# A rotary-embedding score kernel rewritten in emission order: three VectorE operations per rotation, no GpSimd, 4 MB stores, paired loads

## The chip, the cores and the metric

The kernel runs on one core of one Trainium2 chip. The metric is the device time of one execution in microseconds (us). The kernel before takes 897.9 us in the median of 4 runs (897.11 to 898.37). An execution with the profiler on lasts about as long as one without; "span" is the time from its first to its last instruction.

Some words that recur: a packet is one of the pieces (4 to 32 KB here) in which the core's 16 DMA engines move a transfer, and the trace has the start and duration of each; the ring is the queue in which transfers wait in the order of their issue; a transfer has landed when its last engine has reported completion; a stage is a buffer in SBUF (the core's on-chip memory) in which a step's output is collected before it is stored; PSUM is the memory into which TensorE writes, in banks; the granted clock is the share of TensorE's full clock rate that the profile shows.

## The reference

```python
batch, seq, heads, dim = 16, 512, 16, 64          # q, k: float32; cos, sin: [seq, dim/2]
q_rot = concat([q1*cos - q2*sin, q1*sin + q2*cos])   # q1, q2: the halves of dim
k_rot = the same of k
scores = einsum('bshd,bthd->bsht', q_rot, k_rot)     # [16, 512, 16, 512] float32
```

The output is 268.4 MB, the inputs 67.1 MB. A step of the kernel makes one batch's scores for 128 rows of q: 1 MB of loads (k and q, for later steps) and 4 MB of stores. There are 64 steps.

## The kernel before

Tiles come from pools, and a scheduler chooses each engine's order. q is rotated on VectorE and k on GpSimd, with six instructions of 128x512 each:

```python
kq_pool = ctx.enter_context(tc.tile_pool(name="kq", bufs=3))
stage_pool = ctx.enter_context(tc.tile_pool(name="stage", bufs=2))
...
return [lambda: eng.tensor_tensor(o1, x1, cb, op=mult),   # eng: vector for q, gpsimd for k
        lambda: eng.tensor_tensor(tmp, x2, sb, op=mult),
        lambda: eng.tensor_tensor(o1, o1, tmp, op=subtract),
        ...                                              # three more for o2
```

In each step, 16 matmuls go through four PSUM banks, ScalarE copies each bank to one of two 2 MB stages, and the transposes for the next steps come after them:

```python
rope_k = k_rope(rope_target(i), nc.gpsimd)
rope_q = q_rope(i + 2, nc.vector)
k_dma(rope_target(i + 2))            # nc.sync.dma_start, 512 KB
q_dma(i + 4)                         # nc.sync.dma_start, 512 KB
for h in range(H):
    nc.tensor.matmul(out=psm, ...)
    _cp(nc.scalar, sta[:, h, :], psm)                 # or stb
    ...  # after h = 7 and h = 15: nc.sync.dma_start of 2 MB
run_all(rope_k); run_all(rope_q)
do_transposes(specs, (nc.vector, nc.scalar))          # 16 transposes, 16 copies of 128x128
```

All transfers are issued by SyncE, so they stand in one ring in the order of issue.

## Time and profile before

| before | value |
|---|---|
| time, span | 897.9 us, 900.3 us |
| all DMA packets, sum over 16 engines / 16 | 840.7 us |
| DMA idle, span less that sum | 59.6 us |
| of it before the first store packet at 64 us | 39.1 us |
| load packets: 4 KB, median and mean | 159, 188 ns |
| store packets: 16 KB, median and mean | 611, 627 ns |

### The profile page before, as it was taken

The numbers are of one execution on the slowest core, as the hardware profiler recorded it, in microseconds if no ns is written. First come the engines' busy times: TensorE is split into PE (matmuls) and PEld (weight loads), VectorE is DVE, ScalarE is ACT, GpSimd is POOL, SyncE is SP. The second block draws the span as 40 slices with busy tenths as digits, with TensorE's granted clock in tenths as the row PEclk, the third lists the DMA queues.
The fourth block names the chain that finished last, engine by engine and source line by source line (L and its number), as shares of the span: only waits on it lengthen the run. The fifth ranks groups of instructions, "written<-read, shape, count | busy, mean of one in ns | idle before, by whom it ended". The sixth has DMA issues, their size and how long they took to land.

```text
span 900.3 us, 9994 instructions
## 1 busy us (share of the span) xinstructions
PE 718.8 (80%) x3072; PEld 408.7 (45%) x3072; DVE 573.8 (64%) x908; ACT 623.2 (69%) x1537; POOL 555.2 (62%) x378
## 2 busy tenths in 40 slices
PE   0367988987868878887988888888878988888994
PEld 0234544544535544444544544444445545545552
DVE  4997864454347776776775767775576566786500
ACT  0136977876757776766766867767767767767994
POOL 6993667655656766865866766777567674773000
PEclk9997999999989998999999989989989988989997
DMA  4358999999999999999999999999999998998998
GB/s 159 103 183 323 405 418 414 412 398 407 399 401 363 398 385 380 397 405 380 393 379 381 393 380 406 427 416 381 397 397 359 405 392 359 389 416 364 399 415 363
DMA packets 38068, 336.32 MB, mean 374 GB/s; under 512 B 5248, under 2 KB 5248, under 8 KB 21632
## 3 DMA queue, kind: packets, MB, share of 16 engines
q1 hardware_dynamic: 38016, 335.69, 93.1%
q8 instruction: 25, 0.41, 0.2%
q14 instruction: 27, 0.22, 0.1%
HBM read 67.24 MB, written 268.44 MB: 373 GB/s over the span
## 4 chain that ended last, share of the span: by engine, by line
DMA 40%; POOL 28%; PE 12%; DVE 10%; ACT 7%; issue 1%; SPq 1%; POOLq 0%; ACTq 0%; DVEq 0%
DMA ksb<-in_k_dram 21%; DMA qsb<-in_q_dram 19%; PE psm L205 11%; POOL krot L64 6%; POOL krot L65 6%; POOL krot L62 6%; POOL tmp L66 6%; POOL tmp L63 5%; ACT stb L76 3%; ACT sta L76 3%; DVE tmp L63 2%; PE bank L158 1%; DVE qrot L62 1%; DVE tmp L66 1%; DVE qT_new L78 1%
## 5 line engine op out<-in xcount | busy, mean ns | idle before, releaser
L205 PE MATMUL psm<-kT_new,qT_new 64*128 64x512 f32 x2048 | 592.7, 677 | 133.6 <-DVE qT_new L78 82.1
L205 PEld LDWEIGHTS psm<-kT_new,qT_new 64*128 64x128 f32 x2048 | 294.5, 200 | 393.6 <-ACT sta L76 161.1
L76 ACT COPY sta<-psm 128x512 f32<-128x512 f32 x512 | 267.1, 617 | 28.2 <-PE psm L205 27.5
L76 ACT COPY stb<-psm 128x512 f32<-128x512 f32 x512 | 262.1, 706 | 0.0
L63 DVE TENSOR_TENSOR tmp<-qsb,sin 128x512 f32<-128x512 f32 x64 | 65.4, 1021 | 239.5 <-DMA qsb<-in_q_dram 239.5
L63 POOL TENSOR_TENSOR tmp<-ksb,sin 128x512 f32<-128x512 f32 x62 | 88.6, 1429 | 194.3 <-DMA ksb<-in_k_dram 194.3
L76 ACT COPY qT_new<-bank 128x128 f32<-128x128 f32 x256 | 62.7, 267 | 191.2 <-DVE qT_new L78 190.0
L62 POOL TENSOR_TENSOR krot<-ksb,cos 128x512 f32<-128x512 f32 x62 | 92.1, 1486 | 65.8 <-PE bank L158 58.8
L78 DVE COPY qT_new<-bank 128x128 f32<-128x128 f32 x256 | 67.9, 284 | 53.1 <-PE bank L158 41.3
L65 POOL TENSOR_TENSOR krot<-ksb,sin 128x512 f32<-128x512 f32 x62 | 98.6, 1591 | 0.0
L64 POOL TENSOR_TENSOR krot<-krot,tmp 128x512 f32<-128x512 f32 x62 | 97.2, 1568 | 0.0
L76 ACT COPY kT_new<-bank 128x128 f32<-128x128 f32 x256 | 65.3, 266 | 46.0 <-DVE kT_new L78 45.0
L66 POOL TENSOR_TENSOR tmp<-ksb,cos 128x512 f32<-128x512 f32 x62 | 93.6, 1509 | 4.6
L67 POOL TENSOR_TENSOR krot<-krot,tmp 128x512 f32<-128x512 f32 x62 | 92.2, 1487 | 3.8
L158 PE MATMUL bank<-ident,krot 128*128 128x128 f32 x512 | 70.0, 282 | 28.0 <-POOL krot L67 18.3
L65 DVE TENSOR_TENSOR qrot<-qsb,sin 128x512 f32<-128x512 f32 x64 | 88.1, 1377 | 0.0
L67 DVE TENSOR_TENSOR qrot<-qrot,tmp 128x512 f32<-128x512 f32 x64 | 83.9, 1311 | 1.6
L66 DVE TENSOR_TENSOR tmp<-qsb,cos 128x512 f32<-128x512 f32 x64 | 82.8, 1293 | 0.0
L158 PEld LDWEIGHTS bank<-ident,qrot 128*128 128x128 f32 x512 | 55.5, 142 | 56.2 <-issue 56.2
L64 DVE TENSOR_TENSOR qrot<-qrot,tmp 128x512 f32<-128x512 f32 x64 | 80.7, 1261 | 0.0
L158 PE MATMUL bank<-ident,qrot 128*128 128x128 f32 x512 | 70.8, 282 | 8.1 <-DVE qrot L67 8.1
L158 PEld LDWEIGHTS bank<-ident,krot 128*128 128x128 f32 x512 | 60.6, 145 | 29.1 <-POOL krot L67 18.7
(15 smaller groups left out, 155.2 us busy)
## 6 DMA issues: line engine op xcount, KB each, us to landing
out_dram<-sta SPq DMA_DIRECT2D x64, 2048.0 KB, 10.0
out_dram<-stb SPq DMA_DIRECT2D x64, 2048.0 KB, 13.4
ksb<-in_k_dram SPq DMA_DIRECT2D x64, 512.0 KB, 5.8
qsb<-in_q_dram SPq DMA_DIRECT2D x64, 512.0 KB, 13.6
cos<-in_cos_dram SPq DMA_DIRECT2D x4, 16.0 KB, 1.8
sin<-in_sin_dram SPq DMA_DIRECT2D x4, 16.0 KB, 1.8
```

What stands on the lines that cost most here:

```text
L62: lambda: eng.tensor_tensor(o1, x1, cb, op=mybir.AluOpType.mult),
L63: lambda: eng.tensor_tensor(tmp, x2, sb, op=mybir.AluOpType.mult),
L64: lambda: eng.tensor_tensor(o1, o1, tmp, op=mybir.AluOpType.subtract),
L65: lambda: eng.tensor_tensor(o2, x1, sb, op=mybir.AluOpType.mult),
L66: lambda: eng.tensor_tensor(tmp, x2, cb, op=mybir.AluOpType.mult),
L67: lambda: eng.tensor_tensor(o2, o2, tmp, op=mybir.AluOpType.add),
L76: nc.scalar.copy(out=dst, in_=src)
L78: eng.tensor_copy(out=dst, in_=src)
L158: nc.tensor.transpose(slot, inap, ident)
L205: nc.tensor.matmul(out=psm, lhsT=qT[64 * r : 64 * r + 64, hp, :], rhs=kT[64 * r : 64 * r + 64, hp, :, :], start=True, stop=True,)
```

## The change

The intent: let program order fix every engine's order; make fewer, larger instructions and transfers; keep more output in flight. The core of the diff, with cuts:

```diff
-    kq_pool = ctx.enter_context(tc.tile_pool(name="kq", bufs=3))
-    rot_pool = ctx.enter_context(tc.tile_pool(name="rot", bufs=3))
+    in_pool = ctx.enter_context(tc.tile_pool(name="in", bufs=2))
+    rot_pool = ctx.enter_context(tc.tile_pool(name="rot", bufs=2))
-    stage_pool = ctx.enter_context(tc.tile_pool(name="stage", bufs=2))
-    psum_t_pool = ctx.enter_context(tc.psum_pool(name="ps_t", bufs=4))
-    psum_m_pool = ctx.enter_context(tc.psum_pool(name="ps_m", bufs=4))
+    stage_pool = ctx.enter_context(tc.tile_pool(name="stage", bufs=3))
+    ps_s_pool = ctx.enter_context(tc.psum_pool(name="ps_s", bufs=3))
+    ps_t_pool = ctx.enter_context(tc.psum_pool(name="ps_t", bufs=2))
+    q_v = q.rearrange("b (p c) h d -> b p c h d", c=C)
+    k_v = k.rearrange("b (c p) h d -> b p c h d", p=P)
+    o_v = out.rearrange("b (p c) h t -> b c p h t", c=C)
 ...  (tables of cos|cos and sin|-sin, loaded from ScalarE's ring)
+        t = in_pool.tile([P, 2, H, D], fp32, tag="k_in", bufs=3, name="k_sb")
+            nc.sync.dma_start(t, k_v[b, :, 2 * pair : 2 * pair + 2])     # 1 MB; q the same, bufs=2
 ...
+            lambda: nc.vector.tensor_tensor(a, src, cc, op=mult),
+            lambda: nc.vector.tensor_tensor(bt, src, ss, op=mult),
+            lambda: nc.vector.tensor_tensor(a4, a4, swapped, op=add),
 ...
+    with tc.manual_schedule():
 ...
+            after = {0: 0, 2: 1, 3: 2, 5: 3}
+            for hp in range(HP):
+                ps = ps_s_pool.tile([P, 2, S], fp32, tag="ps_s")
+                for r in range(2):
+                    nc.tensor.matmul(out=ps[:, r, :], ...)
+                nc.scalar.copy(out=st[:, 2 * hp : 2 * hp + 2, :], in_=ps)
+                if hp in after and after[hp] < len(tr):
+                    rot, g, dst = tr[after[hp]]
+                    bank = transpose_group(rot, g)
+                    if dve:
+                        dve.pop(0)()
+                    nc.vector.tensor_copy(out=dst, in_=bank)
+            for op in dve:
+                op()
 ...  (one 1 MB load: q in odd steps, k in even ones)
+                nc.sync.dma_start(o_v[b, c], st)                          # 4 MB
```

## The prediction

> **What bounds the kernel now.** I read the page first (busy shares, slices, DMA table), then the stretches of time, the packet records, the start of the timeline and the groups of instructions. The slices and the queue table carry most of it:
>
> ```profile
> PE 718.8 (80%) x3072; PEld 408.7 (45%) x3072; DVE 573.8 (64%) x908; ACT 623.2 (69%) x1537; POOL 555.2 (62%) x378
> ...
> DMA  4358999999999999999999999999999998998998
> GB/s 159 103 183 323 405 418 414 412 398 407 399 401 363 398 385 380 397 405 380 393 379 381 393 380 406 427 416 381 397 397 359 405 392 359 389 416 364 399 415 363
> ...
> q1 hardware_dynamic: 38016, 335.69, 93.1%
> ```
>
> No compute engine is above 80%, while the 16 DMA engines are at 90% or more in every slice but the first four and a few late ones that read 8. The chain that ended last is 40% "DMA" and 28% "POOL", which looks like a latency loop (load, GpSimd rotation, buffer free, next load); but the stretches say that the pipe it waits on is full:
>
> ```profile
> core 0: us, PE busy (x) PEld busy (x) DVE busy (x) ACT busy (x) POOL busy (x), PEclk, DMA share, GB/s
> 0.00:60.00 60.00, 20.82 (x72) 13.10 (x72) 47.06 (x49) 13.07 (x36) 52.08 (x38) 1.00 0.37 129
> 60.00:100.00 40.00, 29.55 (x128) 16.78 (x128) 32.96 (x49) 25.08 (x65) 23.08 (x15) 0.83 0.88 337
> 100.00:200.00 100.00, 85.52 (x385) 49.17 (x383) 57.21 (x114) 76.76 (x193) 60.77 (x47) 0.98 1.01 413
> ...
> 400.00:500.00 100.00, 83.04 (x355) 46.39 (x352) 72.00 (x103) 72.48 (x181) 69.52 (x45) 0.95 0.98 387
> ```
>
> The last two columns are the busy share of the DMA engines and the rate. From 100 us on the share is 0.92 to 1.01, so the steady state is DMA time. Idle is in the front: 0.63 x 60 = 38 us and 0.12 x 40 = 5 us. Of the span of 900.3 us, 93.1% or some 838 us is packet time, so about 62 us in all is idle.
>
> The rate at a full share is not constant: 413 GB/s in the second 100 us, 387 between 400 and 500. Counting the packet records by size shows why. The 16,384 store packets of 16 KB have a median of 0.611 us and a mean of 0.627; the 16,384 load packets of 4 KB have a median of 0.159 and a mean of 0.188, with a tail up to 1.6 us. By medians the work would take 16,384 x 0.611 / 16 + 16,384 x 0.159 / 16 = 626 + 163 = 788 us; by means it is 642 + 193 = 835. So 47 us is stretched packets, 30 of them on loads. The long load packets come just after stores. In 100 to 150 us, where work is queued ahead, the loads average 22.6 GB/s per engine; in 400 to 450 us, where the queue runs nearly empty before a load is issued, 18.8.
>
> **What the Trainium skill says.** "VectorE: DVE Perf Modes", section "The TRN2 errata", gives a fp32 tensor_tensor of N elements (N+151)/0.96 ns, so 691 ns at 512. "SBUF — State Buffer", section "Who interferes with whom", says that a VectorE instruction with two SBUF inputs contends with a GpSimd instruction that reads SBUF. The trace has both. The first of these rows has GpSimd waiting for its load, the second has it running:
>
> ```profile
> 410.56 0.69 DVE L63 TENSOR_TENSOR tmp<-qsb,sin 128x512 f32<-128x512 f32 x1 [2.42 <-DMA qsb<-in_q_dram]
> ...
> 403.05 1.75 DVE L65 TENSOR_TENSOR qrot<-qsb,sin 128x512 f32<-128x512 f32 x1
> ```
>
> "DMA: Bandwidth & Descriptors", section "Latency and other measured facts", lists 16 KB rows at a pitch of 512 KiB at nearly full rate and of 2 MiB clearly slower. The new store has 32 KB rows at a pitch of 4 x 32 = 128 KB, which that list does not reach, and the old one had 32 KB pitch, so no run here shows it yet. That all stores and loads share one ring is as it was before, so I give it no gain.
>
> **The change part by part.**
>
> *Rotation.* Six VectorE and six GpSimd instructions of 128x512 per step become six VectorE instructions of 128x1024 (three for q, three for k). Without GpSimd I take the 0.69 us row and add 512 elements at 1/0.96 ns: 1.22 us each, as the page's formula gives (1.224); back to back some 1.17, because the rows of 0.69 follow one another at 0.61. Six are 7.0 us.
>
> *PSUM copies of the transposes.* Sixteen 128x128 copies per step, half on VectorE (0.284 us) and half on ScalarE (0.267), become four 128x512 VectorE copies: 0.284 + 384/0.96 ns = 0.68, say 2.7 us. VectorE's step: 9.7 us.
>
> *Score copies.* Sixteen of 128x512 per step become eight of 128x1024. Now the row
>
> ```profile
> 405.19 4.11 ACT L76 COPY stb<-psm 128x512 f32<-128x512 f32 x8
> ```
>
> gives 0.51 us each. Adding 512 elements at the 0.833 ns of "ScalarE: Activation LUTs", section "Step-by-step: what each stage is for", makes 0.94, and 8 x 0.94 = 7.5 us per step against the 16 x 0.51 = 8.2 plus 2.1 of before. These rows agree only loosely with 0.833: 0.51 less 0.25 (three 128x128 copies in 0.75) over 384 elements is 0.68 ns.
>
> *TensorE.* The same matmuls: 16 at 0.43 us where it is not held by ScalarE (weight loads of 879.94, 880.48, 880.91 follow at that distance), 6.9 us, and 16 transposes at 8 per 1.05 us, 2.1 us. 9 us.
>
> So every engine needs under 10 us per step, and the pieces are interleaved so that they mostly overlap; I expect a compute step of about 10 us.
>
> *DMA.* The same 335.5 MB. From the medians of 4 KB and 16 KB packets a packet costs 8 ns plus 0.0368 ns per byte (an estimate), so 8,192 stores of 32 KB take 1.214 us each, 621 us in all; 8,192 k packets of 4 KB 81 us; 4,096 q packets of 8 KB at 0.310 us, 79 us; about 2 us for semaphores and tables. Floor: 783 us, 5 less than before. That is 12.2 us per step, above the 10 us of compute, so three stages of 4 MB keep one to two stores queued ahead all the time. I therefore use the loss of the stretch with a full queue: 100 to 150 us moves 407 GB/s at a share of 0.996, 409, against 425.5 by medians: 0.961. 783 / 0.961 = 815 us of packet time.
>
> *The start.* The old kernel spends 4.5 us of SyncE issue on eight tables before k; the first k lands at 8.1 us. Now tables go out from ScalarE and k at once: k lands at some 4.3 us, with tables built near 4.6. VectorE then rotates alone: four k chunks 14.0, q tables 1.1, q 3.5, q 3.5, k of the next batch 3.5 us: 30.2 us. Step 0 cannot transpose before that, and its own VectorE work is 9.7 us, so the first store leaves at about 40.5 us. By then 8.4 MB of loads are done, 20.4 us of packets. The end is 40.5 + (815 - 20.4) + 2 for the last landing = 837 us of span. The span of before is 2.6 us longer than the timed median, so 834 us timed. I move it up to 838 since more can stretch than shrink.
>
> So the gain of about 60 us is some 40 us of DMA idle time (62 down to about 22) and some 20 us of packet time (835 down to 815). The shorter rotation itself is worth nothing after the start: it only keeps VectorE alone below the DMA's step.
>
> **Rivals.**
> 1. *The pipe is full anyway and loads stay slow.* A load after each 4 MB store still pays; k and q come in 1 MB bursts, as in 400 to 450 us, where 384.6 GB/s at a share of 0.988 make 389. Then packet time is 783 x 425.5 / 389 = 856, the end 878 us, timed 876: 2.4% faster. For it: the long packets sit in those bursts. Against it: there the queue was nearly empty, and will not be now.
> 2. *VectorE becomes the bound.* All rotation and all transpose copies are on one in-order engine, and its first rotation in each step waits for a q load. If a pair of operations waits for the other engine at each of four transposes, a step of 14 us is thinkable: 40 + 63 x 14 = 922 us, 3% slower. For it: TensorE waits for VectorE at each new step. Against it: 9.7 us leaves 3 us per step, two PSUM banks hold transposes, and each q pair is issued two whole steps (25 us) ahead.
> 3. *The pitch of the stores costs rate.* Each 3% lost on the 621 us of stores is 19 us; 10% would give back all of the gain.
> 4. *Loads ahead of stores in one in-order queue hold the stores*, since a load waits for the last rotation of its step. Both are due at about the same time, and with stores queued behind this costs nothing except at step 0, where it is counted.
>
> **Range and chances.** Full-queue losses between 2% and 7% give packet times of 799 to 842, and with the 20 us of early idle and 2 at the end, times of 819 to 862; I add a little for rivals 1 and 3. Predicted 838 us, 8 in 10 between 818 and 868. Faster by over 2% (under 880): 0.93; within 2%: 0.04; slower: 0.03, rival 2 or a bad pitch.
>
> **What would show it.** DMA share of 0.98 or more from 45 us to the end; the first store issued near 40 us; 32 KB packets at about 1.21 us and 4 KB means near 0.18; VectorE operations of 128x1024 at 1.2 us and VectorE busy near 75%; score copies near 1.0 us each; ScalarE waiting for the landing of a stage, not for TensorE. It is wrong if the DMA share falls below 0.95 in the middle (a compute step over 12.8 us), if 32 KB packets have a median over 1.25 us, or if VectorE waits long for q.

## More of the kernel before

The page of the profile and its stretches are read in the prediction. One view it did not use is the list of waits of the SyncE sequencer itself, which issues the transfers. Of the kernel before (sequencer and line, what it waited for, us in total, times, longest):

```profile
SPq L103 <- POOL tmp L66: 382.9, 42, 11.7
SPq L215 <- ACT sta L76: 182.4, 26, 10.2
```

L103 is the k load. It waits for GpSimd's last reading of an input buffer, 383 us in all, and what stands behind it in SyncE's order waits with it: L215 and L221, the stores, too.

## The result, and the profile after

The changed kernel takes 827.8 us (825.84 to 829.46, 4 runs). Its ratio to the kernel before is 0.9224, with a 95% interval of 0.9204 to 0.9243. A ratio here is the mean time of one kernel's fast runs over that of the other's of the same rounds, so it is not quite the ratio of the medians quoted. The gain is 7.8%.

The page of the changed kernel: busy time by engine, then the slices of TensorE's clock, the DMA's busy share and its rate, and the share of the data queue.

```profile
PE 682.7 (83%) x3072; PEld 298.2 (36%) x3072; DVE 605.9 (73%) x638; ACT 496.4 (60%) x523; POOL 0.7 (0%) x6
...
DMA  8389999999999999999999999999999999999994
GB/s 318 102 315 433 427 415 429 435 422 428 431 429 428 434 430 430 432 430 429 432 432 427 427 433 431 425 438 430 427 433 420 428 430 431 388 404 430 418 419 195
...
q1 hardware_dynamic: 22560, 335.55, 96.0%
```

VectorE now does all the rotation and is busy for 606 us, hardly more than before, and GpSimd for none. The DMA's share is full from the fourth slice to the last but one, and, unlike before, so is its rate: about 430 GB/s in nearly every slice, where before it moved between 359 and 427. The stretches of the changed kernel show it with the numbers (last two columns: DMA share, GB/s):

```profile
0.00:20.00 20.00, 5.82 (x24) 4.70 (x24) 13.30 (x15) 4.21 (x6) 0.70 (x6) 1.00 0.86 328
20.00:45.00 25.00, 18.18 (x68) 9.18 (x68) 21.15 (x25) 10.08 (x13) 0.00 (x0) 1.00 0.25 85
...
400.00:500.00 100.00, 86.44 (x388) 37.56 (x388) 76.89 (x82) 61.32 (x65) 0.00 (x0) 0.95 1.00 429
...
800.00:825.00 25.00, 2.71 (x14) 0.93 (x10) 0.00 (x0) 3.76 (x4) 0.00 (x0) 0.63 0.57 245
```

From 400 to 500 us the share went from 0.98 to 1.00 and the rate from 387 to 429. A full share had not meant full speed. The idle that is left is at the two ends. The packet records give the account of the 74.7 us between the two spans (the medians of the times are 70.1 us apart: the profiled execution of the kernel before was slower than its median):

| us, sum over 16 engines / 16 | before | changed | gained |
|---|---|---|---|
| load packets | 192.9 | 166.7 | 26.2 |
| store packets | 642.5 | 624.3 | 18.2 |
| all packets, with semaphores, tables and fetches | 840.7 | 795.2 | 45.5 |
| DMA idle before the first store packet (at 64 and 49 us) | 39.1 | 22.4 | 16.7 |
| DMA idle after it | 20.5 | 8.1 | 12.4 |
| span, the last three rows together | 900.3 | 825.6 | 74.7 |

Of the packets, larger sizes explain little: at their medians (159 ns for 4 KB, 309 for 8, 611 for 16, 1213 for 32) loads shrink by 2 us and stores by 5. The other 37 us are packets that no longer stretch beyond their median: 4 KB loads average 165 ns where they averaged 188. The kernel before had another order in the ring as well: from 61 to 246 us and from 558 to 730 us its scheduler put loads and stores in turn, and about 11 of the 17 us by which its stores exceed their median lie in these two stretches.

The start of the changed kernel, from the timeline of SyncE (start, us of issue, what), shows where the front is:

```profile
44.61 0.37 SPq L80 DMA_DIRECT2D k_sb<-in_k_dram  x1
45.78 0.36 SPq L209 DMA_DIRECT2D out_dram<-st  x1
48.73 0.34 SPq L87 DMA_DIRECT2D q_sb<-in_q_dram  x1
56.26 0.34 SPq L209 DMA_DIRECT2D out_dram<-st  x1
65.58 0.38 SPq L80 DMA_DIRECT2D k_sb<-in_k_dram  x1
66.75 0.34 SPq L209 DMA_DIRECT2D out_dram<-st  x1
```

The first store leaves at 45.8 us. The next follow 10.5 us apart: that is the compute step with nothing in its way, and it is below the 12.3 us that a step's packets need, so the ring fills. Later the engines wait for the DMA, as the list of waits of the changed kernel says:

```profile
ACT st L194 <- DMA out_dram<-st: 188.9, 55, 4.8
```

ScalarE waited 55 times for the landing of an old stage. SyncE's own waits in the changed kernel are these:

```profile
SPq L209 <- ACT st L194: 363.2, 64, 13.6
SPq L80 <- DVE bt L102: 299.9, 29, 16.4
SPq L87 <- DVE bt L102: 80.3, 30, 7.1
```

The loads wait nearly as long as before, 300 us for k and 80 us for q, while the DMA's share is full from 45 to 700 us. So the sum of such waits does not tell their cost; the experiments look at how much is still in the ring when a wait ends.

The costs of single instructions, from the groups (busy, mean ns of one, idle before):

```profile
L194 ACT COPY st<-ps 128x1024 f32<-128x1024 f32 x512 | 489.3, 1021 | 286.5 <-DMA out_dram<-st 188.9
...
L200 DVE COPY qT_t<-bank 128x512 f32<-128x512 f32 x126 | 87.0, 691 | 145.8 <-PE bank L113 145.1
L103 DVE TENSOR_TENSOR a<-a,bt 128x1024 f32<-128x1024 f32 x128 | 156.2, 1220 | 2.2
```

### The profile page after: what moved, and what is told of

It is laid out like the page before. It is cut to its first block, busy times and chain, and to the rows that moved or that the text cites. A ratio compares the mean times of both kernels' runs of the same rounds, so it can differ in the third digit from the quotient of the medians.

```text
span 825.6 us, 7746 instructions
## 1 busy us (share of the span) xinstructions
PE 682.7 (83%) x3072; PEld 298.2 (36%) x3072; DVE 605.9 (73%) x638; ACT 496.4 (60%) x523; POOL 0.7 (0%) x6
## 4 chain that ended last, share of the span: by engine, by line
DMA 65%; PE 19%; ACT 7%; DVE 5%; issue 1%; ACTq 0%
DMA out_dram<-st 64%; PE ps L187 14%; ACT st L194 7%; PE bank L113 5%; DVE bt L102 2%; DVE a L103 1%; DVE a L101 1%; DMA sin_k_raw<-in_sin_dram 1%; DVE qT_t L200 1%; ACTq L237 0%; ACTq L194 0%; ACTq L53 0%; DVE cc_q L62 0%; DVE ss_k L65 0%; DVE ss_q L65 0%
## 5 line engine op out<-in xcount | busy, mean ns | idle before, releaser
L194 ACT COPY st<-ps 128x1024 f32<-128x1024 f32 x512 | 489.3, 1021 | 286.5 <-DMA out_dram<-st 188.9
L187 PE MATMUL ps<-kT_t,qT_t 64*128 64x512 f32 x2048 | 530.4, 639 | 75.5 <-ACT st L194 75.3
L187 PEld LDWEIGHTS ps<-kT_t,qT_t 64*128 64x128 f32 x2048 | 182.2, 193 | 257.7 <-issue 151.4
L113 PE MATMUL bank<-ident,a 128*128 128x128 f32 x1024 | 178.8, 302 | 44.6 <-DVE a L103 44.6
L113 PEld LDWEIGHTS bank<-ident,a 128*128 128x128 f32 x1024 | 115.9, 149 | 246.1 <-issue 143.6
L200 DVE COPY qT_t<-bank 128x512 f32<-128x512 f32 x126 | 87.0, 691 | 145.8 <-PE bank L113 145.1
L103 DVE TENSOR_TENSOR a<-a,bt 128x1024 f32<-128x1024 f32 x128 | 156.2, 1220 | 2.2
L200 DVE COPY kT_t<-bank 128x512 f32<-128x512 f32 x120 | 82.4, 687 | 25.9 <-PE bank L113 25.7
L101 DVE TENSOR_TENSOR a<-q_sb,cc_q 128x1024 f32<-128x1024 f32 x64 | 77.9, 1217 | 0.0
L102 DVE TENSOR_TENSOR bt<-k_sb,ss_k 128x1024 f32<-128x1024 f32 x64 | 77.8, 1215 | 0.0
L102 DVE TENSOR_TENSOR bt<-q_sb,ss_q 128x1024 f32<-128x1024 f32 x64 | 77.6, 1213 | 0.0
L144 ACT COPY kT_t<-bank 128x512 f32<-128x512 f32 x8 | 4.7, 586 | 15.3 <-PE bank L113 15.3
```

The costliest lines, as they stand in the source:

```text
L101: lambda: nc.vector.tensor_tensor(a, src, cc, op=mult),
L102: lambda: nc.vector.tensor_tensor(bt, src, ss, op=mult),
L103: lambda: nc.vector.tensor_tensor(a4, a4, swapped, op=add),
L113: nc.tensor.transpose(bank[:, n, :], rot[:, 2 * hp : 2 * hp + 2, :], ident)
L144: nc.scalar.copy(out=k_dst(0, c, g), in_=bank)
L187: nc.tensor.matmul(out=ps[:, r, :], lhsT=qT[i][64 * r : 64 * r + 64, hp, :], rhs=kT[b][64 * r : 64 * r + 64, hp, :, :], start=True, stop=True,
```

## The experiments

The question is what made packets stop stretching and the ring stay full. My theory is the depth of the ring: how much is queued when a load is issued. Rivals are the size of packets, the number of changes between loads and stores, the absence of GpSimd, and the pitch of the rows. Three parts of the change were not undone alone, so what each is worth is not shown: the program order itself, the rotation in three instructions instead of six, and the larger score copies. All runs gave correct results, and each is compared by its ratio to the kernel before of the same rounds. "Packets" is the sum over the 16 engines divided by 16; "idle after" is DMA idle after the first store packet. (The expectations were written with a first count that took an instruction fetch for that packet, so they say 11 us for the changed kernel where the table says 8.)

| run | median us | ratio (95%) | packets us | 4 KB mean ns | store mean ns (size) | idle after us |
|---|---|---|---|---|---|---|
| changed kernel | 827.8 | 0.9224 (0.9204-0.9243) | 795.2 | 165 | 1219 (32 KB) | 8.1 |
| two stages | 869.2 | 0.9663 (0.9606-0.9720) | 818.3 | 207 | 1221 (32 KB) | 27.9 |
| alternating halves | 852.2 | 0.9509 (0.9474-0.9545) | 816.4 | 165 | 627 (16 KB) | 8.3 |
| halves, loads first | 836.2 | 0.9310 (0.9262-0.9358) | 803.5 | 166 | 614 (16 KB) | 8.0 |
| store halves only | 833.5 | 0.9295 (0.9240-0.9351) | 800.9 | 171 | 613 (16 KB) | 9.0 |
| rows as before | 829.4 | 0.9248 (0.9220-0.9276) | 797.1 | 165 | 1218 (32 KB) | 7.6 |
| k on GpSimd | 831.2 | 0.9270 (0.9239-0.9300) | 793.8 | 162 | 1220 (32 KB) | 7.3 |
| before, five input buffers | 862.9 | 0.9597 (0.9546-0.9649) | 817.1 | 169 | 623 (16 KB) | 10.8 |

### Two output stages

```diff
-    stage_pool = ctx.enter_context(tc.tile_pool(name="stage", bufs=3))
+    stage_pool = ctx.enter_context(tc.tile_pool(name="stage", bufs=2))
```

> The changed kernel with two output stages instead of three. Theory (queue depth: load packets stretch when the ring is nearly empty as they are issued): with two stages only one 4 MB store and a load, 12.3 us of packets, stand in the ring while the next stage takes some 10 us to fill, so the ring runs close to dry at each step. Packet time rises from 795 us to 805-825, the mean of the 4 KB load packets from 165 ns to 175-200, idle after the first store from 11 us to 15-40, time 835-865 us. Rival (packet size, or one load per step instead of two): packet time stays at 793-797 and load packets at 165 ns; only idle time may grow.

Measured: 869.2 us and 4 KB loads of 207 ns, both a little past the theory's numbers; packets of 818.3 us and idle of 27.9, both within them. More than half of the gain is gone with one buffer, and the load packets stretch again (24.5 us over their median, against 3.1 in the changed kernel), though their size and order are the same. It is k's 4 KB packets that stretch; q's of 8 KB average 325 ns against 321 in the changed kernel. The time of issue fits the theory: from 100 to 700 us, the last earlier transfer landed 3.3 us in the mean after a k load was issued, and 13.1 us after a q load. (k's and q's packets also differ in size, and this run does not separate the two.) The slices of this run show it between 343 and 431 GB/s at a share that reads 9 in all but one of them:

```profile
DMA  8289999999999999999989999999999999999997
GB/s 302 97 354 420 431 404 417 403 417 382 375 422 431 412 424 407 370 397 386 395 343 418 429 381 378 416 396 385 365 383 425 421 376 387 401 387 389 410 416 335
```

### The kernel before with deeper input buffers

```diff
-    kq_pool = ctx.enter_context(tc.tile_pool(name="kq", bufs=3))
+    kq_pool = ctx.enter_context(tc.tile_pool(name="kq", bufs=5))
```

> The kernel before with five instead of three buffers for q and k inputs and nothing else; a k load then no longer waits for GpSimd to free a buffer at the head of the SyncE ring, where stores stand behind it (that wait is 383 us in all in the kernel before). Theory (the in-order ring is held by that wait, so it runs dry and loads meet an empty ring): SyncE's wait for GpSimd falls below 100 us, packet time from 840 to 800-820 us, time from 898 to 860-880. Rivals (rotation work, packet sizes or ScalarE made the gain): time stays at 890-900.

Measured: 862.9 us, 4.0% faster than the kernel before, with its GpSimd rotation, its 16 KB stores, its small copies. Packets fell from 840.7 to 817.1 us and the 4 KB mean from 188 to 169 ns. SyncE's wait for GpSimd fell to 154 us, less far than I said. q's buffers grew too, so that VectorE's wait for q loads fell from 240 to 34 us. The waits of SyncE in this run, largest first:

```profile
SPq L221 <- ACT stb L76: 237.8, 63, 7.0
SPq L215 <- ACT sta L76: 202.4, 41, 10.0
SPq L103 <- POOL tmp L66: 154.3, 25, 10.7
```

So half of the gain was one number away in the old kernel: a load that waited for GpSimd stood before finished stores in SyncE's order. Near 405 us of the kernel before, the last copy into a stage ended at 405.4 us, and its store was issued at 408.1 us, behind the k load.

The edit is not pure: the scheduler also changed SyncE's order. In both kernels some stretches have loads and stores in turn and others have k, q and then two stores, but at different times. This can be used, for stretches of the same order can be compared. "Ahead" is the mean time from the issue of a k load to the landing of the last transfer issued before it; all numbers are of one profiled execution each:

| run, stretch | order | ahead us | 4 KB mean ns | store mean ns |
|---|---|---|---|---|
| before, 300 to 500 us | loads together | 2.7 | 210 | 616 |
| five buffers, 150 to 300 us | loads together | 14.4 | 160 | 613 |
| before, 600 to 700 us | in turn | 9.2 | 169 | 648 |
| five buffers, 400 to 500 us | in turn | 19.3 | 163 | 638 |

Loads stretch where little is ahead of them, in the same order; stores stretch where loads and stores alternate, with either depth.

### Alternating loads and stores

```diff
-                nc.sync.dma_start(t, ...)            # one load of 1 MB
-                nc.sync.dma_start(o_v[b, c], st)     # one store of 4 MB
+            for x in range(2):
+                nc.sync.dma_start(t[:, x], src[bl, :, 2 * pl + x])
+                nc.sync.dma_start(o_v[b, c, :, 8 * x : 8 * x + 8, :], st[:, 8 * x : 8 * x + 8, :])
```

> The changed kernel with every 1 MB load cut into two of 512 KB and every 4 MB store into two of 2 MB, issued in turn (load, store, load, store), so two changes of direction per step and 16 KB store packets and 4 KB load packets as before the change. Theory (queue depth): the ring stays as full, so packet time rises only by the size term, 788 instead of 783 us of floor, to about 800, 4 KB mean below 172 ns, time 828-838 us. Rival (turns or sizes made the gain): packet time goes back toward 825-840 us and time to 855-870.

Measured: 852.2 us. The theory missed by 14 us, and the rival by 3. The loads stayed short (165 ns), as the theory says; it is the stores that stretched, to 627 ns in the mean for a median of 611, which is 17 us in all. Three things were changed at once here, so two more runs took them apart. The first halves only the stores and issues both at the end:

```diff
-                nc.sync.dma_start(o_v[b, c], st)
+                for x in range(2):
+                    nc.sync.dma_start(o_v[b, c, :, 8 * x : 8 * x + 8, :], st[:, 8 * x : 8 * x + 8, :])
```

> The changed kernel with each 4 MB store cut by heads into two of 2 MB that are issued one behind the other, so store packets of 16 KB but loads of 1 MB and one change of direction per step as in the changed kernel. The run with alternating halves took 24 us more, 17 of them from store packets longer than their median. If the smaller store packet is the cause: 16 KB mean near 628 ns again, packet time 812-818 us, time 846-854. If the second change of direction per step is the cause: mean below 616 ns, packet time about 800 us, time 831-837.

Measured: 833.5 us and 613 ns. The size of the packet costs its 5 us of floor, and no more that this run can tell. The second keeps all of the alternating run's transfers and changes their order:

```diff
             for x in range(2):
                 if t is not None:
                     nc.sync.dma_start(t[:, x], src[bl, :, 2 * pl + x])
+            for x in range(2):
                 nc.sync.dma_start(o_v[b, c, :, 8 * x : 8 * x + 8, :], st[:, 8 * x : 8 * x + 8, :])
```

> The run with alternating halves, with only the order changed: the same two loads of 512 KB and two stores of 2 MB per step, but both loads first and both stores behind them (load, load, store, store), so one change of direction per step; number, sizes and 8-deep semaphore limit of the DMAs are as in the alternating run (852 us, 16 KB packets 628 ns in the mean). If alternation stretched the stores: 16 KB mean below 616 ns, packet time 800-803 us, time 831-838. If the number of DMAs or the split loads did it: 16 KB mean near 628 ns, time 847-855.

Measured: 836.2 us and 614 ns. Between this run and the alternating one nothing differs but the order, and it is worth 16 us. (The "semaphore limit" of the expectation: SyncE's transfers share eight semaphores, and it waited some 75 times in each of the two runs for an earlier store to land.) A second change of direction per step stretches the stores, as it did in the old kernel's stretches above. Why it is the stores that pay, no run shows.

### Rows as before, and k on GpSimd

Two parts of the change were undone alone. First the mapping of rows:

```diff
-    q_v = q.rearrange("b (p c) h d -> b p c h d", c=C)
+    q_v = q.rearrange("b (c p) h d -> b p c h d", p=P)
-    o_v = out.rearrange("b (p c) h t -> b c p h t", c=C)
+    o_v = out.rearrange("b (c p) h t -> b c p h t", p=P)
 ...  (and q's tables in the same mapping)
```

> The changed kernel with q and the output mapped as before (128 neighbouring rows per chunk): store rows of 32 KB at a pitch of 32 KB instead of 128 KB, q packets of 4 KB instead of 8. My theory gives the interleaved rows nothing but q's larger packets: packet time within 2 us of 795 plus 2, time 826-832 us. Rival (the 128 KB pitch costs): stores become faster than 1219 ns on average and time falls below 822. Rival (larger q packets matter): time above 835.

Measured: 829.4 us, stores of 1218 ns against 1219. A pitch of 128 KB costs nothing, and q's 8 KB packets gain at most 2 us. Then the engine of k's rotation:

```diff
-            lambda: nc.vector.tensor_tensor(a, src, cc, op=mult),      # and the two after it
+            lambda: eng.tensor_tensor(a, src, cc, op=mult),            # eng = nc.gpsimd for k, b > 0
-        bt = rot_pool.tile([P, H, D], fp32, tag="part", bufs=2)
+        bt = rot_pool.tile([P, H, D], fp32, tag="part_" + which, bufs=1)
```

> The changed kernel with k's three rotation instructions of 128x1024 put on GpSimd for all batches but the first. Theory (the DMA sets the step; the engine of the rotation matters only where its step passes 12.3 us or where a load waits for it): GpSimd needs about 3 x 3.1 us = 9.3 us per step, VectorE's three are slowed to 2-3 us each by sharing, under 12.3 us both; time within 1% of the changed kernel, 826-836 us, most of any loss at the first store. Rival (taking GpSimd out made the gain): time above 850 us.

Measured: 831.2 us. VectorE's instructions take longer while GpSimd's run, as the groups of this run show (the mean in ns is the last number before the second bar):

```profile
L103 POOL TENSOR_TENSOR bt<-k_sb,ss_k 128x1024 f32<-128x1024 f32 x60 | 199.4, 3323 | 1.2 <-DVE a L104 1.2
...
L104 DVE TENSOR_TENSOR a<-a,bt 128x1024 f32<-128x1024 f32 x68 | 182.5, 2685 | 0.2
```

A VectorE instruction goes from 1.22 to 2.69 us, the first store leaves at 52.0 us instead of 45.8, and the time changes by half a percent. "No GpSimd" by itself is worth about nothing here.

### More VectorE work

```diff
-                dve += ops
+                dve += ops[:1] + ops                 # two more per step (one for q, one for k)
+                dve += ops[:1] + ops[:2] + ops[1:]   # the other run: four more per step
```

> The changed kernel with two more 128x1024 VectorE multiplications per step (the first of each rotation done twice; 2.4 us more, VectorE's step about 12.1 us with its copies). Theory: VectorE is off the path as long as its step stays below the DMA's 12.3 us, so time is 826-838 us. Rival (each rotation instruction removed is worth its time): 64 x 2.4 = 150 us more, 980 us.

> The changed kernel with four more 128x1024 VectorE multiplications per step: VectorE's step is then 9.9 + 4 x 1.16 = 14.5 us, above the DMA's 12.3, so VectorE should set the step: 63 x 14.5 + 46 + some 12 for the end = 960-990 us by the theory, VectorE busy above 93%, DMA share below 0.9. If time stays below 900, VectorE's step is shorter than I count.

Measured: 908.3 us (ratio 1.0126) and 1109.0 us (1.2361). Both missed, and so did the rival's 980 us. With two more, VectorE's own work is what I counted, 747 us busy over 64 steps or 11.7 us a step, but two stores that are two steps apart leave at 404.9 and 432.2 us, 13.7 us a step. The waits of that run (two more instructions) say why:

```profile
PE bank L113 <- DVE a L103: 186.9, 65, 12.0
...
DVE kT_t L200 <- PE bank L113: 66.9, 60, 2.9
```

TensorE waits for the last rotation of the step before it can transpose, then VectorE waits for that transpose. The step is VectorE's work plus about 2 us of such waits, so the room below the DMA's 12.3 us was never the 3 us that the prediction took from VectorE's 9.7 alone; the changed kernel's 10.5 us step leaves 1.8. With four more it is 16.9 us, (1108.3 - 45) / 63, with VectorE busy for only 81%. TensorE's granted clock was 0.81 in this run, where it was 0.95 in the changed kernel; what part of the longer step that makes, no run separates. In both runs the step is longer than the DMA's 12.3 us, the ring runs dry (in the first of them, from 100 to 700 us, k loads are issued 2.0 us before the last earlier landing), and the 4 KB loads stretch to 244 and 242 ns in the mean: the depth theory again, from another side.

### An earlier first store

```diff
-            after = {0: 0, 2: 1, 3: 2, 5: 3}
+            after = {4: 0, 5: 1, 6: 2, 7: 3} if i == 0 else {0: 0, 2: 1, 3: 2, 5: 3}
                 nc.scalar.copy(out=st[:, 2 * hp : 2 * hp + 2, :], in_=ps)
+                if i == 0 and hp % 2 == 1:
+                    nc.sync.dma_start(o_v[b, c, :, 2 * hp - 2 : 2 * hp + 2, :], st[:, 2 * hp - 2 : 2 * hp + 2, :])
 ...  (and no 4 MB store in step 0)
```

> The changed kernel with a shorter way to the first store: step 0 does its transposes for later steps after the fifth to eighth instead of the first to sixth pair of heads, and its output leaves in four stores of 1 MB as each fourth is copied. Theory (about 20 us of DMA idle before the first store at 45.8 us is what is left): first store at 31-34 us, time 9-14 us shorter, 813-819 us. Rival (what starts early is lost to a later stall of steps 1 to 3): time 824-828.

Measured: 823.4 us (ratio 0.9188, 0.9155 to 0.9221, which overlaps the changed kernel's 0.9204 to 0.9243). The first store left at 31.9 us as expected, but the time missed: about 4 us of the 14 came through. Some 5 us of idle returned between 50 and 55 us, where the ring waited for all of step 1's output. A second form also cuts step 1's store in four and loads k's tables before k:

```diff
-                if i == 0 and hp % 2 == 1:
+                if i < 2 and hp % 2 == 1:
 ...  (and no 4 MB store in steps 0 and 1)
-                nc.scalar.dma_start(t, src.rearrange(pat, **kw))
+                (nc.sync if which == "k" else nc.scalar).dma_start(t, src.rearrange(pat, **kw))
```

> The run with the earlier first store, with the output of step 1 also in four stores of 1 MB, and the two tables for k issued on the SyncE ring before k itself. It left 5 us of DMA idle between 50 and 55 us, where the ring waited for the whole of step 1's output, and the first rotation waited 2 us for the sine table behind k's packets. Theory: both go; first store at about 30 us, idle between 50 and 60 us below 1 us, time 815-819. If early idle only moves later, 822-825.

Measured: 820.3 us, ratio 0.9137 (0.9100 to 0.9174), whose interval lies clear of the changed kernel's. This is the fastest version found. It misses its forecast by a little: idle between 50 and 60 us fell to 0.1 us as expected, but 3.4 us of idle turned up between 60 and 70 us. Its slices begin 8, 7, 8 where the changed kernel's begin 8, 3, 8:

```profile
DMA  8789999999999999999999999999999999999994
```

### The straggler at the end

The last slice reads 4 in both. By the packet records, 16 packets are in work at any time until about 814 us in the changed kernel, then fewer, and from 816.6 to 824.2 us one at a time: one engine works alone for 7.6 us (the expectation below says 9). This tail holds nearly all of the 8.1 us of idle after the first store. The semaphore landings show when it fell behind. Between the landing of the eighth of the 16 engines and the last, a transfer that ends near 100 us has 2.3 us, near 400 us 7.3, near 700 us 13.6. In the kernel before the gap stays below 5 us, for its ring runs dry and the engines meet again; with five input buffers the gap rises to 15.6 us. After 45 us the trace has 23 instruction fetches of 16 KB and 12 of 8 KB, 35 in all. Of the 8192 store packets, 25 are 0.29 to 0.42 us longer than the median, and 24 of these overlap one of the fetches. (The expectation below says that each fetch has one, which is too much.)

```diff
+    pad = const_pool.tile([P, 1], fp32, name="pad")
 ...
+            for _ in range(50):
+                nc.gpsimd.memset(pad, 0.0)           # 128x1; nothing reads it
```

> The changed kernel with 50 small memsets per step on the idle GpSimd, 3200 instructions and some 205 KB of instruction fetch more, and nothing that waits for them. In the changed kernel a single DMA engine works alone for the last 9 us. Theory: it is the one that also carries the instruction fetches (22 packets of 16 KB after 45 us, each with one data packet stretched by about 0.4 us beside it). If the added fetches come on the same engine, the lone tail grows by 5-8 us and time to 832-837; if on another engine, a second engine trails and time stays at 826-830 us. Rival (the straggler has nothing to do with fetches): tail and time as before, one engine alone for 9 us.

Measured: 846.9 us (ratio 0.9436), 19 us slower, from 3200 instructions on an engine that nothing waits for. The gap grew about twice as fast, to 13.9 us near 400 us, and then stayed between 13 and 17 us to 730 us. I read this as the other engines having worked off what was queued and waiting for the slow one; load packets stretched once more (184 ns), and idle after the first store was 15.3 us. GpSimd's memsets did not slow VectorE: its 128x1024 instructions took 1.22 us as before. So it fits that instruction fetches slow one engine and that a full ring then runs at the pace of its slowest; that it is the fetches, and nothing else about a busy GpSimd, no run separates. My forecast missed in size and in kind: the time one engine worked alone at the end did not grow (6.1 us). 23 more fetches of 8 KB are 7 us by their own packets. What the rest of the 19 us is stays open, and so does which engine it is, since the trace does not label packets with engines.

## Why the prediction was right

**The total.** 838 was forecast, 818 to 868 as the range, and 827.8 was measured. The mechanism held: DMA-bound before and after, a compute step of about 10 us (10.5 measured) below the packets' 12.2, and a gain made of less idle and fewer stretched packets.

**Instruction costs.** VectorE's 128x1024 came out at 1.22 us as worked out, its 128x512 copy at 0.69 (0.68), ScalarE's 128x1024 at 0.92 apart (0.94; 1.02 long). The page "VectorE: DVE Perf Modes" and the trace agree; 1.0 to 1.7 us before, beside GpSimd, was for half as many elements.

**Packet time, 815 forecast, 795 measured.** The floor of 783 was right to within 1 us (the medians of the 8 and 32 KB packets came out at 309 and 1213 ns). The mis-sized term is the loss, 3.9% taken from the kernel before's best stretch; with a ring that is never near dry it is 1.4%. Even that best stretch was not free of stretched packets: its loads and stores came in turn, with 4 KB packets of 182 ns and stores of 618 in the mean (89 to 139 us by the right dates).

**The stretches of packets were dated 11 us wrong.** The packet records count from 11 us before the first instruction, and I had not seen it. With the right dates, loads are 172 ns in 100 to 150 us and 214 ns in 400 to 450, so the contrast in size stands. But I took it for one of depth alone, and the two stretches differ in order too: loads and stores in turn in the first, loads together in the second. That depth is the cause for the loads is shown only by the experiments, above all by the four stretches compared under the kernel with five buffers.

**The start, 40.5 us forecast, 45.8 measured.** The first rotation began at 7.2 us, not 4.6: the sine table, on ScalarE's ring, landed only at 7.0, behind k's packets. And step 0 took 13.3 us after the last rotation instead of 10.3, because TensorE's weight loads followed one another at 0.85 us until 36 us, where I had used the 0.43 of a later stretch.

**The end, 2 us forecast.** It has the straggler, one engine alone for 7.6 us, which no view that I read of the kernel before could show, since its engines meet again at each dry moment.

**Span and time.** I took 2.6 us off the span, and the sign was wrong: in every execution that has both, the time is 1.7 to 1.9 us above the span (827.4 and 825.6 us in the changed kernel's profiled run). The profiled execution of the kernel before has no time of its own, but its span alone, 900.3 us, is above all four times, so it was a slower one. A span of 837 us would have meant a time of 839; that I moved 834 up to 838 for another reason hid this by luck.

**The split.** I put 40 us of the gain on idle and 20 on packets; it was 29.2 and 45.5. With 22 us of idle where there were 30, and 815 us of packets where there were 795, the two errors partly cancel, which is luck.

**The rivals.** Rival 1 names something real, but the burst alone does not stretch loads: in the same order they take 210 ns with 2.7 us of work ahead and 160 with 14.4, and in the changed kernel, in bursts of 1 MB, 165. Rival 2 is nearer than I said: 2.4 us more of VectorE work per step and it sets the time. Rival 3 is ruled out by the run with rows as before. Rival 4 happens (SyncE waited 300 us for VectorE before k loads, with stores next in order), and with the ring full it cost nothing that the DMA's share of 1.00 would show. "The shorter rotation is worth nothing" needs a limit: no experiment undid it alone, and a VectorE step that grew by 2.4 us lost 80 us.

## What to carry to other kernels

Where a DMA's busy share is already near 1.0, look at the rate beside it, and at how much is still queued when the issuing sequencer issues a load: a share of 0.98 hid 10% of lost rate, and five input buffers instead of three gave half of this gain. In this kernel it paid to keep one to two stores queued behind the one in flight, to keep loads together instead of between stores, and to have enough buffers, of input or of output, that the ring has not run dry when a load that had to wait for an engine is issued. A compute engine that is "off the path" has only the room that is left after the waits between engines in its loop, so measure that room before spending it.

## What the Trainium skill lacked or had wrong

- "DMA: Bandwidth & Descriptors" rates a transfer by its size and says nothing of how much is in the ring when it is issued: with the same transfers, 4 KB load packets take 165 ns in the mean with three output stages and 207 with two.
- The same page does not tell of alternation: the same transfers in the order load, store, load, store take 852 us, and in the order load, load, store, store 836, with 16 KB store packets of 627 and 614 ns.
- The same page, section "Where 436 GB/s comes from", says that for HBM transfers the HBM side, about 358 GB/s, binds. The changed kernel, on one core, moved 429 GB/s from 400 to 500 us. (The page's own table has 425 GB/s for a core whose pair is idle, and about 358 each when both stream, so it is that one sentence that is too general.) No run here has a second core streaming.
- The same page's list of row pitches begins at 512 KiB; here 32 KB rows at 128 KB cost nothing (1219 ns against 1218 at 32 KB).
- "Runtime: NRT & Kernel Launch", section "Instruction fetch mechanics", calls the cost of a refill mostly hidden. In a kernel bound by DMA, 3200 instructions on an otherwise idle engine cost 19 us, of which 7 us are the fetches' own packets (an estimate, 23 x 309 ns) and the rest is open. The page says blocks of 16 KiB; the fetches that these instructions added came in packets of 8 KB.
- No page has how far the 16 DMA engines drift apart under a full ring: 13.6 us between the middle and the last engine near 700 us. "DMA: Bandwidth & Descriptors" says only that two of the 16 are usually slower, with no size.
